# Moving row gathers between the stages of a hybrid decoder layer on one Trainium2 core

## The chip, the cores and the metric

The kernel runs on one core of one Trainium2 chip. The core has a matrix engine (TensorE, PE in the profile, with its weight load PEld), a vector engine (VectorE, DVE), a scalar engine (ScalarE, ACT), GpSimd (POOL) and a queue engine (SyncE, SP). The metric is device microseconds (us) of one execution, as the median of several runs; lower is better.

## The reference

One decoder layer is applied to 512 prompt tokens and to 64 sample tokens (8 sequences of 8). Cut to what matters here:

- `proj = x @ w_in` gives q, k, v, u and two gates. Sliding-window attention runs on q, k, v and a state-space branch on u.
- `mix = sigmoid(ga) * (a @ w_attn_proj) + sigmoid(gb) * (s @ w_ssm_proj)`, then `x = LN1(alpha * x + mix @ w_out)`.
- `peer`: for each token, 8 heads choose 16 of 16,384 experts by product keys (`q = x @ w_q`, two top-16 lists, the top 16 of their sums). With the chosen indices, `h = gelu(x . u_tab[idx])` and `y = sum(g * h * v_tab[idx])`. Then `x = LN2(alpha * x + y)`.
- A last gated addition, `x = x + sigmoid(x @ w_gate) * (p @ w_proj)`.

All tensors are float32.

## The kernel before

**Two groups of tokens.** Group A is the 64 sample tokens (block 0) and the first 128 prompt tokens (block 1). Group B is the other 384 prompt tokens (blocks 2, 3 and 4). Group A goes through attention, state space, output product, norm and expert choice first; group B follows stage by stage.

**Two ways to do the experts.** For group B the expert layer is dense: all 128 "columns" of 128 experts are multiplied on TensorE, first `u` (`up`, L1143), then, weighted by a grid of gates, `v` (L1288). For group A only the chosen rows are read: GpSimd gathers one row of the table for each of the 128 partitions (`gathered`, L1077), and VectorE makes one pass over it, a product with a sum for `u_tab` (L1087) or a multiply-add into `acc` for `v_tab` (L1096). Block 1 has 128 rows of each table, block 0 has 64 of each: 384 row steps, in one fixed order (block 1 u, block 1 v, block 0 u, block 0 v). Four buffers hold gathered rows (`gt`, 4), so a gather waits until the pass four rows earlier is done.

**How row steps are placed.** `rows` is that chain of row steps and `pull(n)` adds n to a running debt and performs a row step for each whole unit of it. Each stage of group B calls `pull` at its own steps. The constants say how much each call asks for: `PG` in the gated linear unit (`glu`, 4 steps), `P0` beside the attention product (`mix0`, 8 steps), `P1` beside the state-space product (`mix1`, 8 steps), `P4` beside the output product (`out`, 8 steps, L655), `P2` beside the norm (`ln1`, 3 steps), `P3` beside the expert query (`peerq`, 4 steps, L426), `PULL1` beside each of the first 50 u columns (`first`). In `dense` 78 columns do u and v together and ask for `PULL3` each (in three thirds), and the last 50 do only v and ask for `PULL4` each.

**What sets the order.** The instructions of an engine are issued in one order fixed at compile time by a planner; the passes over rows are pinned (`pin`) behind what was traced before them on VectorE, other instructions can move forward. The matrix engine works on float32 as a high and a low part (`split`, `parts`): ScalarE copies the high part (L214), VectorE subtracts to get the low part (L217, `wl`, `ul`, `vl`), and three products are summed. The first `W1` = 8 columns of `first` take the raw float32 table instead, with no split. Beside the columns of `first`, two steps per column of `side` run on VectorE: the close of the top-k of block 2 (11 steps), 8 empty steps, 17 steps of its gate grid, and the same for blocks 3 and 4. So the side work is done after about 47 columns.

**The tail.** After the dense stage each block is normed and goes through the gate product (`ple`, L1383), in the order 1, 2, 3, 4, 0. Before the norm of block 0 there are six calls `pull(2)` and then, in `norm(0)`, `pull(1000)`, which performs all row steps that are left; then `acc` of block 0 is folded on TensorE (L1102), added (L1103) and normed.

```
tail = (1, 2, 3, 4, 0)
norm(2)
for i, bi in enumerate(tail):
    pull(PULL5)
    if i + 2 < 5 and tail[i + 2]:
        norm(tail[i + 2])
    next(todo[bi])
    pull(PULL6)
    if i == LASTN:
        norm(0)
...
```

Of the kernel before, what the change touches and what calls it, by code (L numbers as in the profile page):

```python
# [36 lines left out]
E0 = 50  # L37
EB, KB, TB = 2, 2, 2
BQ, ABG, AB0, AB1, AB2 = 2, 0, 1, 1.5, 2
P0, P1, P2, P3, P4, PG = 0.75, 1.5, 3, 2, 1.5, 1  # L40
YFIRST = True
QK0, QK1 = (4, 0, 1), (2, 3)
SIDE = 2
# [3 lines left out]
W0, W1, WHOLEQ, DEEP = 0, 8, 1, 2  # L47
# [6 lines left out]
T0, T1, T2 = 0.5, 1, 1  # L54
LATE = 0
AHEAD = 3
PULL1, PULL3, PULL4, PULL5 = 0.75, 3, 1, 2

# [140 lines left out]
def build(tc, I, O, dbg=None):  # L201
# [17 lines left out]
    with (  # L219
# [889 lines left out]
        def pull(n):  # L1109

            due[0] += n
            while due[0] >= 1:
                due[0] -= 1
                while rows and next(rows[0], rows) is rows:
                    rows.pop(0)
# [11 lines left out]
        def up_parts(e2, du, whole=False, deep=3):  # L1127

            raw = du.tile([128, D], FP, tag="ur", name="ur", bufs=3)
            SY.dma_start(raw, I["u_t"][e2].rearrange("p c e -> p (c e)"))  # L1130
            return (raw,) if whole else split(du, raw, D, "u", deep)

        def up(e2, u, x, hp, tag="gl", bufs=5, lanes="AB"):

            xh, xl, xr = x
            p = ps(384, lanes[e2 % len(lanes)])
            if len(u) == 1:
                terms = ((u[0], xr, True, True),)
            else:
                terms = ((u[0], xh, True, False), (u[0], xl, False, False), (u[1], xh, False, True))  # L1140
            for w, z, f, l in terms:
                for c in range(8):
                    T.matmul(p, w[:, c * 128:c * 128 + 128], z[:, c], start=f and c == 0, stop=l and c == 7)  # L1143
            gl = hp.tile([128, 384], FP, tag=tag, name="gl", bufs=bufs)
            act(gl, p, AF.Gelu)
            return gl
# [59 lines left out]
        def first(du, hp, oh, x, topk):  # L1206

            io16 = oh.tile([128, 128, 2], F16, name="io16")
            V.tensor_copy(io16, iota[:, :, None].to_broadcast([128, 128, 2]))

            def side():
                for b in range(3):
                    while 2 + b not in GW:
                        next(topk, 0)
                        yield

                    for _ in range(LAG[b]):
                        yield
                    yield from grid(b, oh, io16)

            work = side()
            def parts_of(e2):
                return up_parts(e2, du, W0 <= e2 < W1, DEEP)


            u = parts_of(0)
            for e2 in range(E0):
                u, now = parts_of(e2 + 1) if e2 + 1 < E0 else None, u
                if e2 < KEEP:
                    H0[e2] = up(e2, now, x, hp, "keep", KEEP, lanes="A")  # L1230
                else:
                    SY.dma_start(Hd[e2], up(e2, now, x, hp, lanes="A"))
                for _ in range(SIDE):
                    next(work, 0)
                pull(PULL1)
            for _ in work:
                pull(PULL1)

# [309 lines left out]
        with tc.tile_pool(name="hp", bufs=1) as hp:  # L1548
            with tc.tile_pool(name="du", bufs=1, reuse_waits="tile") as du, tc.tile_pool(name="oh", bufs=1) as oh:
                first(du, hp, oh, x, B.topk(tk, (0, 1, 2)))  # L1550
            xrs.close()
            tks.close()
            du2 = ExitStack()
            du = open_(du2, "du2", 1, "right", reuse_waits="tile")

            def last():
                du2.close()
                xB.close()
                return finish(open_(fin, "fin", 1, "right"))

            dense(du, hp, x, last)
# [17 lines left out]
```

## Time and profile before

| | |
|---|---|
| median of 3 runs | 1870.27 us (1869.79 to 1870.85) |
| profiled execution, its own time | 1867.68 us |
| its span, first to last instruction | 1865.9 us |
| mean granted TensorE clock | 0.979 |
| PE busy | 1791.8 us (96%) |
| DVE busy | 1451.8 us (78%) |
| ACT busy | 756.8 us (41%) |
| POOL busy | 575.1 us (31%) |

The profile is of one execution. An engine's busy time is the sum of its instructions' times; what matters for an edit is the engine that ends a wait in the stage where the edit is. A granted clock of 1.0 is TensorE's upper level (2.4 GHz), 0.5 the lower (1.2 GHz); a stretch in between has some time at each.

### The profile page before, as it was taken

The numbers are of one execution on the slowest core, as the hardware profiler recorded it, in microseconds if no ns is written. First come the engines' busy times: TensorE is split into PE (matmuls) and PEld (weight loads), VectorE is DVE, ScalarE is ACT, GpSimd is POOL, SyncE is SP. The second block draws the span as 40 slices with busy tenths as digits, with TensorE's granted clock in tenths as the row PEclk, the third lists the DMA queues.
The fourth block names the chain that finished last, engine by engine and source line by source line (L and its number), as shares of the span: only waits on it lengthen the run. The fifth ranks groups of instructions, "written<-read, shape, count | busy, mean of one in ns | idle before, by whom it ended". The sixth has DMA issues, their size and how long they took to land.

```text
span 1865.9 us, 26455 instructions
## 1 busy us (share of the span) xinstructions
PE 1791.8 (96%) x9506; PEld 1539.1 (82%) x9506; DVE 1451.8 (78%) x2878; ACT 756.8 (41%) x1135; POOL 575.1 (31%) x409
## 2 busy tenths in 40 slices
PE   8799999999989989999999999999999999899997
PEld 6778987767769678889889999999999998688885
DVE  7553343796769999899778888888888887898885
ACT  1213452242243259697743333333333333443331
POOL 0110000032321121112245655555555554542230
PEclk9898999999999989999999999999999999999998
DMA  8824564167883469898999999999999999999952
GB/s 254 302 97 140 157 225 161 58 220 242 307 324 139 148 209 286 276 310 285 304 381 375 387 338 340 348 337 348 337 344 346 334 327 343 402 368 365 337 165 82
DMA packets 212226, 515.43 MB, mean 276 GB/s; under 512 B 33536, under 2 KB 101648, under 8 KB 211568
## 3 DMA queue, kind: packets, MB, share of 16 engines
q1 hardware_dynamic: 145648, 301.68, 46.5%
q0 software_dynamic: 56160, 204.78, 30.2%
q10 hardware_dynamic: 10288, 7.30, 1.3%
q8 instruction: 74, 1.21, 0.3%
q14 instruction: 56, 0.46, 0.1%
HBM read 463.31 MB, written 51.89 MB: 276 GB/s over the span
## 4 chain that ended last, share of the span: by engine, by line
PE 51%; issue 15%; DVE 14%; DMA 11%; POOL 7%; ACT 2%; SPq 0%; ACTq 0%; POOLq 0%; DVEq 0%
PE psA L1288 9%; PE psB L1288 9%; POOL g L1077 7%; PE psA L1143 7%; PE psA L419 6%; PE psB L1143 5%; DMA g<-u_tab,idx 4%; PE psA L426 3%; DMA g<-v_tab,idx 3%; DVE eq L217 3%; PE psB L419 2%; DVE scr L1087 1%; DVE ul L217 1%; PE psA L655 1%; ACT Gs L211 1%
## 5 line engine op out<-in xcount | busy, mean ns | idle before, releaser
L1077 POOL DMA_INDIRECT g<-u_tab,idx x192 | 274.0, 1427 | 792.5 <-DVE scr L1087 485.2
L1077 POOL DMA_INDIRECT g<-v_tab,idx x192 | 282.5, 1471 | 325.9 <-DVE acc L1096 259.8
L1087 DVE SCALAR_TENSOR_TENSOR scr<-g,x 128x1024 bf16<-128x1024 f32 x192 | 233.9, 1218 | 27.0 <-DMA g<-u_tab,idx 25.9
L1096 DVE SCALAR_TENSOR_TENSOR acc<-g,hh,acc 128x1024 f32<-128x1024 f32 x190 | 243.2, 1280 | 10.6 <-DMA g<-v_tab,idx 9.1
L214 ACT ACTIVATE uh<-ur 128x1024 fp32r<-128x1024 f32 x120 | 126.7, 1062 | 163.8 <-PE psA L1143 68.6
L214 ACT ACTIVATE vh<-vr 128x1024 fp32r<-128x1024 f32 x128 | 135.9, 1061 | 96.7 <-PE psB L1288 88.0
L217 DVE TENSOR_TENSOR ul<-ur,uh 128x1024 fp32r<-128x1024 f32 x120 | 146.0, 1217 | 29.7 <-ACT uh L214 29.7
L214 ACT ACTIVATE wh<-wt 128x384 fp32r<-128x384 f32 x128 | 67.1, 524 | 233.5 <-PE psB L1288 200.5
L217 DVE TENSOR_TENSOR vl<-vr,vh 128x1024 fp32r<-128x1024 f32 x128 | 155.9, 1218 | 4.2 <-ACT vh L214 4.2
L1288 PE MATMUL psA<-vh,wh 128*128 128x512 f32 x384 | 150.5, 392 | 8.5 <-ACT wh L214 8.5
L1288 PE MATMUL psA<-vl,wh 128*128 128x512 f32 x384 | 150.7, 393 | 0.0
L1288 PE MATMUL psB<-vl,wh 128*128 128x512 f32 x384 | 150.7, 392 | 0.0
L1288 PE MATMUL psB<-vh,wh 128*128 128x512 f32 x384 | 150.1, 391 | 0.0
L1288 PE MATMUL psB<-vh,wl 128*128 128x512 f32 x384 | 149.9, 390 | 0.0
L1288 PE MATMUL psA<-vh,wl 128*128 128x512 f32 x384 | 149.5, 389 | 0.0
L217 DVE TENSOR_TENSOR wl<-wt,wh 128x384 fp32r<-128x384 f32 x128 | 71.2, 556 | 96.1 <-PE psB L1288 88.4
L1143 PE MATMUL psA<-xh,ul 128*128 128x384 f32 x648 | 132.7, 342 | 4.5 <-DVE ul L217 4.5
L1143 PE MATMUL psA<-xh,uh 128*128 128x384 f32 x648 | 134.3, 346 | 2.5 <-ACT uh L214 2.4
L419 PE MATMUL psB<-xTB,w 128*128 128x384 f32 x400 | 133.7, 486 | 0.0
L1143 PE MATMUL psA<-xl,uh 128*128 128x384 f32 x648 | 128.5, 338 | 0.0
L1143 PEld LDWEIGHTS psA<-xh,uh 128*128 128x128 f32 x648 | 115.9, 192 | 7.8 <-ACT uh L214 3.6
L1143 PEld LDWEIGHTS psA<-xh,ul 128*128 128x128 f32 x648 | 113.8, 190 | 7.4 <-DVE ul L217 5.8
(367 smaller groups left out, 3534.4 us busy)
## 6 DMA issues: line engine op xcount, KB each, us to landing
ur<-u_t SPq DMA_DIRECT2D x128, 512.0 KB
vr<-v_tab SPq DMA_DIRECT2D x128, 512.0 KB
G<-Gg SPq DMA_DIRECT2D x33, 768.0 KB
Gg<-Gs SPq DMA_DIRECT2D x12, 2048.0 KB
w<-w_in SPq DMA_DIRECT2D x42, 512.0 KB
w<-w_q SPq DMA_DIRECT2D x32, 512.0 KB
Hd<-gl SPq DMA_DIRECT2D x48, 192.0 KB
gl<-Hd SPq DMA_DIRECT2D x48, 192.0 KB
```

What stands on the lines that cost most here:

```text
L211: S.activation(out, in_, fn, **k)
L214: S.activation(out, in_, AF.Copy)
L217: return (e or V).tensor_tensor(out, a, b, op=op)
L419: T.matmul(out, w[:, k, :], x[:, k, :], start=(k == 0), stop=(k == kc - 1))
L426: T.matmul(out, a[:, k], b[:, k], start=f and k == 0, stop=l and k == kc - 1)
L655: T.matmul(p[bi][:n], a[:, k + i, c0:c0 + n], b[:, i], start=f and i == 0, stop=e and i == 1)
L1077: G.indirect_dma_start(out=t, out_offset=None, in_=I[tab], in_offset=bass.IndirectOffsetOnAxis(ap=IDX[bi][:, i:i + 1], axis=0))
L1087: pin(V.scalar_tensor_tensor(scr, t, 1.0, X1[bi], op0=mult, op1=mult, accum_out=hh[:, i:i + 1]))
L1096: pin(V.scalar_tensor_tensor(acc, t, hh[:, i:i + 1], acc, op0=mult, op1=add))
L1143: T.matmul(p, w[:, c * 128:c * 128 + 128], z[:, c], start=f and c == 0, stop=l and c == 7)
L1288: T.matmul(y[b][hf], x[:, bs], z[:, hf * 512:hf * 512 + 512], start=f, stop=l)
```

## The change

Five constants change, and in `first` the row steps beside the u columns become conditional.

```diff
-P0, P1, P2, P3, P4, PG = 0.75, 1.5, 3, 2, 1.5, 1
+P0, P1, P2, P3, P4, PG = 1, 1.5, 1, 2, 1, 1
...
-PULL1, PULL3, PULL4, PULL5 = 0.75, 3, 1, 2
+PULL1, PULL3, PULL4, PULL5 = 1, 3, 1, 2
...
                 for _ in range(SIDE):
                     next(work, 0)
-                pull(PULL1)
+
+                pull(PULL1 if e2 >= W1 + 4 else 0)
             for _ in work:
                 pull(PULL1)
```

The attention product asks for 1 row step per step instead of 0.75, the output product for 1 instead of 1.5, the norm for 1 instead of 3. Beside the u columns 0 to 11 no row step is asked for, beside columns 12 to 49 one each instead of 0.75. Nothing else changes: the 384 row steps and their order are the same.

## Rows read from the trace of the kernel before

**Rows 1.** The page's list of engines: busy us, share of the span, instructions.

```profile
PE 1791.8 (96%) x9506; PEld 1539.1 (82%) x9506; DVE 1451.8 (78%) x2878; ACT 756.8 (41%) x1135; POOL 575.1 (31%) x409
```

**Rows 2.** Busy time by stretch: PE, PEld, DVE, ACT, POOL, granted clock, DMA share, GB/s.

```profile
418.00:474.00 56.00, 55.73 (x218) 39.45 (x217) 33.08 (x53) 12.43 (x20) 16.52 (x13) 1.00 0.74 246
493.00:513.00 20.00, 18.01 (x65) 14.40 (x66) 16.47 (x27) 3.40 (x3) 7.31 (x7) 0.83 0.86 275
533.00:545.00 12.00, 4.69 (x21) 3.96 (x21) 4.98 (x8) 3.65 (x4) 3.81 (x4) 0.88 1.01 400
545.00:580.00 35.00, 35.00 (x203) 33.98 (x202) 25.04 (x106) 12.32 (x17) 3.35 (x2) 0.94 0.47 180
666.00:716.00 50.00, 43.36 (x279) 41.57 (x278) 50.00 (x128) 29.24 (x34) 10.63 (x7) 0.86 0.63 210
716.00:930.00 214.00, 205.26 (x1535) 188.28 (x1534) 191.96 (x299) 171.77 (x264) 43.17 (x28) 0.99 0.90 297
```

**Rows 3.** Timeline of PE, output product: start, us, engine, line, operands, [idle before <- releaser].

```profile
494.99 1.22 PE L655 MATMUL psA<-wl,mh 128*128 128x512 f32 x2 [2.94 <-DVE wl L217]
...
501.13 0.67 PE L655 MATMUL psA<-wl,mh 128*128 128x512 f32 x2
```

**Rows 4.** Timeline of DVE, output product: passes over rows, and the low part.

```profile
477.27 1.22 DVE L1087 SCALAR_TENSOR_TENSOR scr<-g,x 128x1024 bf16<-128x1024 f32 x1
...
478.53 1.23 DVE L1087 SCALAR_TENSOR_TENSOR scr<-g,x 128x1024 bf16<-128x1024 f32 x1
...
490.22 1.23 DVE L1087 SCALAR_TENSOR_TENSOR scr<-g,x 128x1024 bf16<-128x1024 f32 x1 [2.16 <-DMA g<-u_tab,idx]
...
493.72 1.22 DVE L217 TENSOR_TENSOR wl<-w,wh 128x1024 fp32r<-128x1024 f32 x1
```

**Rows 5.** Timeline of PE, then DVE, at the start of the expert query.

```profile
543.79 1.65 PE L426 MATMUL psA<-xh,wl 128*128 128x384 f32 x4 [5.68 <-DVE wl L217]
...
541.36 1.23 DVE L1087 SCALAR_TENSOR_TENSOR scr<-g,x 128x1024 bf16<-128x1024 f32 x1 [2.52 <-DMA g<-u_tab,idx]
...
542.51 1.22 DVE L217 TENSOR_TENSOR wl<-w,wh 128x1024 fp32r<-128x1024 f32 x1
```

**Rows 6.** Timeline of ACT there: high parts, and the load that one waited for.

```profile
533.94 1.05 ACT L214 ACTIVATE wh<-w 128x1024 fp32r<-128x1024 f32 x1
...
538.47 1.06 ACT L214 ACTIVATE wh<-w 128x1024 fp32r<-128x1024 f32 x1 [3.48 <-DMA w<-w_q]
```

**Rows 7.** Timeline of PE after the eight raw u columns.

```profile
672.71 2.93 PE L1143 MATMUL psA<-xh,ul 128*128 128x384 f32 x8 [3.26 <-DVE ul L217]
...
693.20 0.59 PE L1174 MATMUL psB<-oa,o 128*128 128x128 f16 x4 [3.38 <-DVE oa L217]
```

**Rows 8.** Waits between 716 and 930: us, times, longest.

```profile
DVE ul L217 <- ACT uh L214: 13.8, 5, 5.3
```

**Rows 9.** Groups on DVE between 1790 and 1830: count, busy, mean ns, idle before.

```profile
L1096 DVE SCALAR_TENSOR_TENSOR acc<-g,hh,acc 128x1024 f32<-128x1024 f32 x12 | 15.4, 1279 | 0.8 <-DMA g<-v_tab,idx 0.7
```

**Rows 10.** Timeline of POOL: a gather beside the norm, and the last gather.

```profile
527.09 0.94 POOL L1077 DMA_INDIRECT g<-u_tab,idx  x1 [16.06 <-DVE scr L1087]
...
1817.29 0.94 POOL L1077 DMA_INDIRECT g<-v_tab,idx  x1 [0.30 <-issue]
```

**Rows 11.** Timeline of DVE: passes after these two gathers, and block 0's norm.

```profile
533.09 1.23 DVE L1087 SCALAR_TENSOR_TENSOR scr<-g,x 128x1024 bf16<-128x1024 f32 x1 [0.43 <-DMA g<-u_tab,idx]
...
1827.01 1.28 DVE L1096 SCALAR_TENSOR_TENSOR acc<-g,hh,acc 128x1024 f32<-128x1024 f32 x1 [0.74 <-DMA g<-v_tab,idx]
...
1838.26 1.28 DVE L1067 SCALAR_TENSOR_TENSOR x<-x,rs,nb 128x1024 f32<-128x1024 f32 x1
```

**Rows 12.** Timeline of PE around the fold of block 0.

```profile
1828.35 3.78 PE L1102 MATMUL psB<-acc,c_fold 128*128 128x512 f32 x4 [1.81 <-DVE acc L1096]
...
1838.98 1.98 PE L1383 MATMUL psA<-w_gatel,th 128*128 128x512 f32 x8
...
1858.03 1.98 PE L1383 MATMUL psB<-w_gateh,tl 128*128 128x512 f32 x8
```

## Prediction

> **What bounds the kernel now.** I read the page first: TensorE (PE) is busy 1791.8 us of the 1865.9 us span [rows 1], so the edit can win only where PE waits or runs at the lower clock, and can lose wherever a new wait reaches PE. Then the busy time by stretch, to find those places. PE is nearly full beside the attention and state-space products, where VectorE has 17 us to spare in 56 (418 to 474). It is not full in three stretches beside which row steps stand today [rows 2]: the output product (493 to 513: PE 18.0 of 20, clock 0.83), the start of the expert query behind the norm (533 to 545: PE 4.7 of 12; then clock 0.94 for 35 us), and the first split u columns (666 to 716: PE 43.4 of 50, clock 0.86, VectorE 50.0 of 50). Last the timelines of these stretches and of the tail, to see which instruction ended each wait.
>
> The reader is to see one pattern. PE's wait ends with a VectorE instruction (`wl`, `ul`, `oa`) that had its input long before and stood behind passes over gathered rows. In the output product PE waits 2.94 us for `wl` and runs slowly until about 501 [rows 3]; in front of that `wl` stands a pass that itself waited for its gather [rows 4]. In the query PE waits 5.68 us for a `wl` that starts at 542.51, though its high part was there at about 535; a pass that waited 2.52 us for its gather stands between [rows 5, 6]. Behind the raw columns PE waits 3.26 us for `ul` and 3.38 us for `oa` [rows 7].
>
> **How many row steps move.** From the constants: before, glu 4, attention 8 x 0.75 = 6, state space 12, output 12, norm 9, query 8, u columns 50 x 0.75 = 37.5, dense 78 x 3 + 50 = 284; together 372.5. The tail's six calls of 2 add 12, which is 384.5 for 384 steps, and the trace shows just 12 passes in the tail [rows 9]: `pull(1000)` finds nothing. After: 4 + 8 + 12 + 8 + 3 + 8 + 38 + 284 = 365, plus 12 is 377. Seven row steps are left for `pull(1000)`, in front of the fold of block 0. So the edit does two things: it clears VectorE's queue at three places, and it puts seven gathers with their passes into the tail.
>
> **Cost, part by part.** A u pass takes VectorE 1.26 us from start to start [rows 4], a v pass 1.28 [rows 9]. Each moves 128 x 1024 floats, 0.52 MB, from GpSimd's queue.
>
> *Attention product, two more steps:* 2.5 us of VectorE, in front of a stretch with 17 us (VectorE's) and more of cover [rows 2]. Zero; without that cover 2.5.
>
> *Output product, four fewer:* until the late `wl` the number done is the same 28 (4 + 8 + 12 + 4 against 4 + 6 + 12 + 6), but two of them now run earlier, in spare time, so the ring of four gathers is no longer drained and the wait of 2.16 us before `wl` goes. PE's 2.94 us and about 2.5 us of slow running (0.17 of the clock over the stretch's first 15 us) go: I take -5, at least -1, at most -5.5.
>
> *Norm, six fewer:* 7.6 us of passes and their waits leave the queue in front of the query's first `wl`. It can then start at 535, when its input is there. PE's 5.68 us and 0.06 of 35 us, 2.1 us, are to be had; next late is the load of the following `w_q`, which ScalarE awaited 3.48 us [rows 6]; six gathers of 0.52 MB fewer, while the DMA engines were full at 400 GB/s [rows 2], bring it earlier. I take -7, between -2 (that load binds) and -7.8.
>
> *Columns 0 to 11, nine fewer:* 11.3 us of VectorE where VectorE is never idle. PE's loss there is 6.6 us idle and 0.14 of 43 us, 6 us: 12.7. The first wait goes with its slow running; the second shrinks only by what VectorE gains over PE, which arrives earlier too. I take -8, between -4 and -12.
>
> *Columns 12 to 49, 9.5 more:* 12 us of VectorE, 5 MB of gathers. From 716 to 930 VectorE has 22 us to spare of 214 and PE 9 [rows 2]; much of VectorE's spare time comes from waiting for ScalarE's high parts [rows 8] and can take passes, but it is not spread evenly. The bounds are 0 and 12; I take +3, a quarter, since the largest waits there are not VectorE's making.
>
> *The tail, seven more:* pulled in one go, they stand in VectorE's pinned order between the last pass at 1827.01 and the fold at 1828.35 [rows 11, 12]. The ring has four buffers: the thirteenth gather can't start before the ninth pass is done, and so on. From a gather's start to its pass, where the pass waited for the data, the trace shows 6.0 us (527.09 to 533.09) and 9.7 us (1817.29 to 1827.01) [rows 10, 11]. Chaining seven steps through four buffers with 6.0 us ends the last pass 12.6 us later than now, with 9.7 us 20.0 us later; at VectorE's own pace, 7 x 1.28, it would be 9.0. I take 14.5, that of 7 us, because little else loads in the tail. PE is in order, and now does half a block of the gate product behind the fold [rows 12]. While it waits it can at most do what needs neither the fold nor the norm of block 0; the chain from fold to the end of that norm is 11.1 us (1828.35 to 1839.5) and block 0's own products 11, so no more than some 4.5 us of the delay can be won back. I take 3: +11.5, between +4.5 and +20.
>
> The Trainium skill speaks for a cheaper tail: DMA: Bandwidth & Descriptors, section "Anatomy of one DMA — SWDGE (gpsimd) path", gives a gather issued by GpSimd 2.0 us and its bytes at 436 GB/s, an estimate of 3.2 us for 0.52 MB. By that the flush would go at VectorE's pace (the first rival below). The trace doesn't agree: 6.0 us is the shortest wait shown here.
>
> **Sum.** -5 - 7 - 8 + 3 + 11.5 = -5.5 us. The profiled execution took 1867.68 us, with 1.8 us around its span; the median of the runs is 2.6 us above it. 1867.7 - 5.5 = 1862.2, and on the median 1864.8: **1865 us**.
>
> **Rivals.**
> 1. *The flush goes at VectorE's pace.* Seven passes at 1.28, less 4.5 won back, is +4.5. For it: only two gathers were in flight at the last wait, and nothing forbids the planner to put other products ahead of the fold. Against it: the 6.0 and 9.7 us. -20 + 3 + 4.5 = -12.5: 1858. Chance 0.14.
> 2. *The tail costs more than the front wins (slower).* The seven gathers land at the tail's 9.7 us and PE's order stays: 20 us of waiting, and 2 more for restarting at the lower clock, as after the waits at 494.99 and 672.71 [rows 3, 7]. -17 + 22 = +5: 1875. It decides as soon as the last pass comes over 17 us later and nothing is won back. Against it: the 9.7 us had an output write beside it. Chance 0.15.
> 3. *The 38 columns become VectorE's.* All 12 us show: -20 + 12 + 11.5 = +3.5, 1874. For it: VectorE is busy 90% there. Against it: its spare 22 us. Chance 0.10.
> 4. *The gain behind the norm isn't there,* since the `w_q` loads end the wait anyway: -2 in place of -7, so -0.5, 1870. Chance 0.11.
>
> My forecast has the rest, 0.50, and by itself lies between 1860 and 1869.
>
> **How the numbers follow.** A measurement of this kernel can tell about 0.2%, 3.7 us, from no change. Four fifths of the forecast's cases and all of the first rival's are faster by more than that: 0.54. The rest of the forecast's (0.10), the fourth rival and the milder ends of rivals 2 and 3 (0.06) lie within it: 0.27. The remaining 0.19 is slower. The range runs from below the first rival, 1856, to just above the second, 1876.
>
> **What would show each step.** In the profile after: no PE wait for `wl` in the output product and at the query's start, and a granted clock near 1 through both; PE arriving at the raw columns about 12 us earlier; the wait for `ul` behind them gone, that for `oa` smaller; dense beginning some 17 us earlier than now; 19 passes instead of 12 in the tail, with a PE wait for `acc` at L1102 of some 10 us in place of 1.81. The prediction is wrong if dense doesn't begin at least 10 us earlier, if the waits only move to another VectorE instruction in the u columns, or if the fold's delay is far from 14 us. The sum is a difference of two larger numbers, 17 and 11.5, so an error of a third in either turns faster into no change.

## The result, and the profile after

The changed kernel takes 1882.41 us (median of 4 runs, 1881.27 to 1884.62), the kernel before 1870.03 beside it: a ratio of 1.0080, 95% interval 1.0063 to 1.0097. The forecast was 1865 us and faster. The profiled execution took 1881.27 us with a span of 1879.5, 13.6 us more than the span before.

The page's list of engines for the kernel after; its line answers to [rows 1]:

```profile
PE 1789.4 (95%) x9506; PEld 1536.5 (82%) x9506; DVE 1453.7 (77%) x2878; ACT 756.7 (40%) x1135; POOL 571.1 (30%) x409
```

The engines do the same work in a longer span, so the 13.6 us are waits of PE. Where they lie is read from busy time by stretch (columns as in [rows 2]), after. PE arrives about 7 us earlier from the output product on, so these stretches are shifted by as much:

```profile
486.00:506.00 20.00, 20.00 (x88) 16.16 (x87) 15.29 (x22) 5.16 (x5) 6.37 (x6) 1.00 0.89 314
528.00:540.00 12.00, 6.07 (x33) 5.75 (x33) 4.66 (x4) 4.08 (x5) 0.00 (x0) 0.94 1.02 401
540.00:575.00 35.00, 35.00 (x198) 33.98 (x198) 20.95 (x103) 11.15 (x16) 0.00 (x0) 0.92 0.25 86
659.00:709.00 50.00, 41.87 (x287) 39.67 (x287) 49.57 (x121) 35.08 (x47) 3.36 (x2) 0.90 0.50 165
709.00:923.00 214.00, 200.18 (x1471) 182.80 (x1469) 194.39 (x298) 163.94 (x249) 54.20 (x36) 0.97 0.91 306
```

The first line is the success: the output product has no gap and the full clock, where it had 18.0 of 20 and 0.83. The `wl` that started at 493.72 [rows 4] now starts at 487.91 (timeline of VectorE), with two passes fewer in front of it. The last pass ahead of it still waits for its gather:

```profile
486.75 1.22 DVE L1087 SCALAR_TENSOR_TENSOR scr<-g,x 128x1024 bf16<-128x1024 f32 x1 [1.58 <-DMA g<-u_tab,idx]
...
487.91 1.22 DVE L217 TENSOR_TENSOR wl<-w,wh 128x1024 fp32r<-128x1024 f32 x1
```

The other stretches are no success: the start of the query still has PE idle for half of 12 us and a clock of 0.92 behind it, the first split u columns are no better than before (41.9 of 50 against 43.4), and in the later columns PE has lost 5 us (200.2 of 214 against 205.3). VectorE is still hardly ever idle in the first split columns (49.6 us of 50), though nine passes in front of them are gone.

The waits themselves, from the timeline of PE after (query, first split columns):

```profile
539.41 1.65 PE L714 MATMUL psB<-w,ev 128*128 128x128 f32 x6 [5.35 <-ACT ev L214]
...
663.37 1.70 PE L1143 MATMUL psA<-xh,uh 128*128 128x384 f32 x8 [3.73 <-ACT uh L214]
...
685.89 0.27 PE L1174 MATMUL psB<-oa,o 128*128 128x128 f16 x1 [2.96 <-DVE oa L217]
```

In [rows 5] and [rows 7] PE waited 5.68 us for `wl` and 3.26 us for `ul`, both VectorE's. Both have gone, and a wait of nearly the same length stands at the same place, now for ScalarE: 5.35 us for `ev`, 3.73 us for `uh`. The timeline of ScalarE after shows what stands in front of these two:

```profile
531.20 1.06 ACT L214 ACTIVATE wh<-w 128x1024 fp32r<-128x1024 f32 x1 [2.67 <-DMA w<-w_q]
535.02 1.06 ACT L214 ACTIVATE wh<-w 128x1024 fp32r<-128x1024 f32 x1 [2.76 <-DMA w<-w_q]
537.93 1.06 ACT L214 ACTIVATE wh<-w 128x1024 fp32r<-128x1024 f32 x1 [1.85 <-DMA w<-w_q]
538.89 0.47 ACT L214 ACTIVATE ev<-psA 128x384 f32<-128x384 f32 x1
...
660.79 1.59 ACT L214 ACTIVATE PFx<-PF 128x1664 uint16<-128x1664 uint16 x1 [5.84 <-DVE PF L1010]
662.28 1.04 ACT L214 ACTIVATE uh<-ur 128x1024 fp32r<-128x1024 f32 x1
```

ScalarE takes its instructions in the order that the planner fixed. `ev`, a copy of 0.47 us, stands behind three high parts that each wait for a load of `w_q`. The first split column's `uh` stands behind `PFx`, a copy for the top-k that waits 5.84 us for VectorE. In the kernel before the same two instructions stand the other way round: the timeline of ScalarE before has that `uh` first and the next `PFx` 7 us behind it.

```profile
663.60 1.06 ACT L214 ACTIVATE uh<-ur 128x1024 fp32r<-128x1024 f32 x1 [0.54 <-DMA ur<-u_t]
...
670.84 1.59 ACT L214 ACTIVATE PFx<-PF 128x1664 uint16<-128x1664 uint16 x1 [5.80 <-DVE PF L1010]
```

In the tail, the timelines of VectorE, GpSimd and PE after answer to [rows 10 to 12]; 19 passes stand there in place of the 12 of [rows 9]:

```profile
1829.25 2.61 DVE L1096 SCALAR_TENSOR_TENSOR acc<-g,hh,acc 128x1024 f32<-128x1024 f32 x2 [0.91 <-DMA g<-v_tab,idx]
1832.90 1.33 DVE L1096 SCALAR_TENSOR_TENSOR acc<-g,hh,acc 128x1024 f32<-128x1024 f32 x1 [1.04 <-DMA g<-v_tab,idx]
1835.62 1.28 DVE L1096 SCALAR_TENSOR_TENSOR acc<-g,hh,acc 128x1024 f32<-128x1024 f32 x1 [1.39 <-DMA g<-v_tab,idx]
...
1839.31 2.60 DVE L1096 SCALAR_TENSOR_TENSOR acc<-g,hh,acc 128x1024 f32<-128x1024 f32 x2 [0.61 <-DMA g<-v_tab,idx]
...
1834.50 0.94 POOL L1077 DMA_INDIRECT g<-v_tab,idx  x1 [0.59 <-DVE acc L1096]
...
1841.97 3.78 PE L1102 MATMUL psB<-acc,c_fold 128*128 128x512 f32 x4 [15.66 <-DVE acc L1096]
```

The fold waits 15.66 us for `acc` in place of 1.81 [rows 12] and comes 13.6 us later. Behind it nothing is won back: from the fold to the end of PE's last product it is 31.6 us after and 31.7 before.

### The profile page after: what moved, and what is told of

Same layout as the page of the kernel before. It is cut to its first block, busy times and chain, and to the rows that moved or that the text cites. A ratio compares the mean times of both kernels' runs of the same rounds, so it can differ in the third digit from the quotient of the medians.

```text
span 1879.5 us, 26465 instructions
## 1 busy us (share of the span) xinstructions
PE 1789.4 (95%) x9506; PEld 1536.5 (82%) x9506; DVE 1453.7 (77%) x2878; ACT 756.7 (40%) x1135; POOL 571.1 (30%) x409
## 4 chain that ended last, share of the span: by engine, by line
PE 49%; issue 3%; ACT 2%; DMA 2%; DVE 2%; POOL 1%; POOLq 0%; DVEq 0%; ACTq 0%
PE psA L1143 13%; PE psA L1289 12%; PE psB L1289 12%; PE psB L1143 8%; ACT Gs L211 1%; POOL g L1077 1%; DMA fr<-w_gate 1%; PE psB L1384 1%; PE psA L1384 1%; PE psB L1175 1%; DMA g<-v_tab,idx 1%; PE psB L1174 1%; ACT ob L211 1%; DMA g<-u_tab,idx 0%; ACT uh L214 0%
## 5 line engine op out<-in xcount | busy, mean ns | idle before, releaser
L1077 POOL DMA_INDIRECT g<-u_tab,idx x192 | 269.2, 1402 | 816.1 <-DVE scr L1087 510.9
L1087 DVE SCALAR_TENSOR_TENSOR scr<-g,x 128x1024 bf16<-128x1024 f32 x192 | 234.5, 1221 | 18.6 <-DMA g<-u_tab,idx 17.4
L214 ACT ACTIVATE wh<-wt 128x384 fp32r<-128x384 f32 x128 | 67.1, 524 | 232.5 <-PE psB L1289 197.5
L1143 PE MATMUL psA<-xl,uh 128*128 128x384 f32 x648 | 133.4, 344 | 0.0
## 6 DMA issues: line engine op xcount, KB each, us to landing
Hd<-gl SPq DMA_DIRECT2D x48, 192.0 KB, 4.2
gl<-Hd SPq DMA_DIRECT2D x48, 192.0 KB, 6.0
```

The lines of the kernel that those rows point to most:

```text
L214: S.activation(out, in_, AF.Copy)
L1077: G.indirect_dma_start(out=t, out_offset=None, in_=I[tab], in_offset=bass.IndirectOffsetOnAxis(ap=IDX[bi][:, i:i + 1], axis=0))
L1087: pin(V.scalar_tensor_tensor(scr, t, 1.0, X1[bi], op0=mult, op1=mult, accum_out=hh[:, i:i + 1]))
```

## The experiments

Most runs move row steps by the same constants; e9, e10 and e13 to e16 also change something else, which their edits show. The table is worked out from the timelines of PE, one profiled execution each: **front** from the first product of the output product to the first raw u product, **u** from there to the first v product, **uv** to the last u product of dense, **v** to the last v product, **fold** to the fold of block 0. All medians are beside a median of before of 1867.0 to 1868.7 us on the same chip (1870.0 for the changed kernel). How far a stage repeats is read from the kernels that leave it as it was: front from 147.9 to 152.5, u from 314.6 to 317.3, uv from 611 to 615 with no link to an edit. So a difference of 3 us or less in u, or of 4 to 5 us or less in front and uv, is not read as an effect.

| kernel | median, ratio [95%] | front | u | uv | v | fold |
|---|---|---|---|---|---|---|
| before | 1870.0 (with after) | 151.4 | 317.2 | 614.4 | 234.1 | 37.5 |
| after | 1882.4, 1.0080 [1.0063, 1.0097] | 144.8 | 326.9 | 611.2 | 235.2 | 50.4 |
| e1_rows_back | 1875.1, 1.0031 [1.0012, 1.0049] | 144.3 | 324.5 | 614.4 | 241.8 | 36.8 |
| e2_tail_alone | 1879.9, 1.0055 [1.0036, 1.0074] | 151.0 | 314.6 | 614.8 | 232.5 | 51.1 |
| e3_front_alone | 1869.4, 1.0003 [0.9990, 1.0015] | 144.5 | 315.8 | 614.1 | 243.1 | 36.8 |
| e4_columns_alone | 1873.4, 1.0027 [1.0009, 1.0044] | 147.9 | 324.0 | 614.1 | 231.2 | 35.5 |
| e5_front_dense | 1861.0, 0.9967 [0.9953, 0.9980] | 144.7 | 316.8 | 614.6 | 233.2 | 36.8 |
| e6_columns_0_11 | 1869.5, 1.0005 [0.9991, 1.0019] | 151.6 | 321.2 | 611.4 | 233.9 | 36.9 |
| e7_columns_12_49 | 1889.7, 1.0124 [1.0103, 1.0144] | 152.1 | 336.2 | 611.1 | 233.5 | 37.0 |
| e8_after_dense | 1870.9, 1.0012 [1.0001, 1.0024] | 144.8 | 323.7 | 613.4 | 233.5 | 36.8 |
| e9_pfx_gpsimd | 1886.8, 1.0108 [1.0085, 1.0131] | 144.2 | 338.2 | 615.0 | 234.4 | 36.8 |
| e10_tail_buffers | 1877.0, 1.0043 [1.0026, 1.0060] | 151.1 | 317.0 | 614.0 | 232.0 | 46.1 |
| e11_tail_half | 1870.7, 1.0015 [1.0001, 1.0029] | 149.7 | 315.1 | 614.2 | 230.8 | 43.0 |
| e12_fewer_in_columns | 1864.8, 0.9977 [0.9968, 0.9987] | 144.5 | 318.0 | 610.9 | 239.5 | 36.8 |
| e13_half_passes | 1870.2, 1.0014 [1.0004, 1.0024] | 152.5 | 321.3 | 610.9 | 233.6 | 37.0 |
| e14_half_gathers | 1864.9, 0.9987 [0.9975, 0.9998] | 150.2 | 318.6 | 610.9 | 235.5 | 36.8 |
| e15_side_later | 1869.9, 1.0004 [0.9990, 1.0018] | 148.3 | 318.5 | 612.1 | 234.5 | 36.8 |
| e16_side_later_best | 1860.7, 0.9959 [0.9944, 0.9974] | 143.1 | 314.6 | 615.0 | 234.0 | 37.1 |
| e17_norm_alone | 1868.0, 0.9998 [0.9980, 1.0017] | 149.5 | 315.8 | 614.5 | 234.4 | 37.1 |
| e18_out_alone | 1862.9, 0.9977 [0.9958, 0.9996] | 144.9 | 317.3 | 613.9 | 234.6 | 36.8 |

**The tail, undone and alone.** On the changed kernel (e1), then on the kernel before (e2):

```diff
-PULL1, PULL3, PULL4, PULL5 = 1, 3, 1, 2
+PULL1, PULL3, PULL4, PULL5 = 1, 3, 1.15, 2
...
-PULL1, PULL3, PULL4, PULL5 = 0.75, 3, 1, 2
+PULL1, PULL3, PULL4, PULL5 = 0.75, 3, 0.86, 2
```

> The changed kernel with PULL4 raised from 1 to 1.15, so that the seven left-over row steps stand beside the last 50 v columns and the tail has its 12 passes again. Theory of the tail (all the loss is the flush of seven rows in front of the fold): the wait for acc at L1102 goes from 15.7 us back to about 2, the fold comes about 13.6 us earlier and the time is 1882.4 - 13.6 = 1869, no change against before. Rival (VectorE has no room in the v columns either): seven passes at 1.28 us push the dense end back by up to 9 us, and the time is 1875 to 1878.

> The kernel before with PULL4 lowered from 1 to 0.86, so that seven row steps are left for the flush in front of the fold, and nothing else. Theory of the tail: the fold waits about 15 us for acc, and the time is 1870 + 13.6 = 1884, as slow as the changed kernel or slower. Rival (the loss comes from the stages in front, and the flush only shows it): a few us, 1871 to 1876.

The tail alone, on an untouched front, makes the kernel slower by 0.55%. Its fold stage grows by 13.6 us, as in the changed kernel (12.9); by the median the loss is 11 us, less than the 14 expected. Putting the seven rows back beside the last 50 v columns takes that away, but the v stage grows by 7.7 us: the rival's price, about 1.1 us a row. Busy time by stretch of the kernel before shows what is full there:

```profile
1560.00:1660.00 100.00, 91.53 (x390) 74.13 (x389) 87.02 (x113) 42.62 (x55) 44.27 (x25) 0.97 1.01 399
```

The DMA engines are at 1.01 and 399 GB/s. Among the waits from 1560 to 1790, ScalarE's for the v table's load was 7.9 us before; with seven more rows (e1) it is:

```profile
ACT vh L214 <- DMA vr<-v_tab: 29.0, 13, 5.1
```

**The front alone, the u columns alone.** Both on the kernel before: e3 takes the three constants of the changed kernel and leaves `PULL1` at 0.75, with eight rows put beside the v columns; e4 takes the edit of the u columns alone (`PULL1` 1 and the condition).

```diff
-P0, P1, P2, P3, P4, PG = 0.75, 1.5, 3, 2, 1.5, 1
+P0, P1, P2, P3, P4, PG = 1, 1.5, 1, 2, 1, 1
-PULL1, PULL3, PULL4, PULL5 = 0.75, 3, 1, 2
+PULL1, PULL3, PULL4, PULL5 = 0.75, 3, 1.16, 2
...
-PULL1, PULL3, PULL4, PULL5 = 0.75, 3, 1, 2
+PULL1, PULL3, PULL4, PULL5 = 1, 3, 1, 2
-                pull(PULL1)
+                pull(PULL1 if e2 >= W1 + 4 else 0)
```

> The kernel before with P0, P2 and P4 of the changed one, PULL1 as before in all 50 columns, and the eight missing row steps put beside the last 50 v columns (PULL4 1.16). Theory that the changed columns give the lead back: the 6.5 us won in the output product last to the end, 1863.5. Rival (the split u columns wait for VectorE whatever comes before, so that an earlier arrival is only waited away): 1868 to 1870.

> The kernel before with the edit of the u columns alone: no row step beside columns 0 to 11, one beside each of the other 38, so that the tail has 11 passes and no flush. Theory that the changed columns give the lead back (the profile after goes from 6.9 us ahead at the raw columns to 2.8 us behind at dense): 9.7 us slower than before at the start of dense, 1879. Rival (the lead is lost in waits that are there without the edit): within 3 us of before, 1867 to 1873. The prediction's own terms, -8 for columns 0 to 11 and +3 for the others, give 1865.

By the median e3 looks like its rival, no gain. Its stages say otherwise: 6.9 us are won in front and kept through u and uv, and 8.9 us are lost in the v columns, where the eight rows went. e4's u stage is 6.8 us longer: the changed columns lose time by themselves, though less than the 9.7 expected.

**The same rows in the first part of dense.** e5 is e3 with the rows moved again; e8 is the changed kernel with its seven rows there.

```diff
-PULL1, PULL3, PULL4, PULL5 = 0.75, 3, 1.16, 2
+PULL1, PULL3, PULL4, PULL5 = 0.75, 3.1, 1, 2
...
-PULL1, PULL3, PULL4, PULL5 = 1, 3, 1, 2
+PULL1, PULL3, PULL4, PULL5 = 1, 3.1, 1, 2
```

> Like the run of the front alone, but the eight missing row steps stand beside the 78 columns of dense that do u and v (PULL3 3.1, PULL4 1). Theory (the front's 6.3 us reach the end unless rows are put where the DMA engines are full, as in the first v columns): the lead of 6.6 us stands at the last u column and at the fold, 1862. Rival (dense has no room either): the eight passes cost 8 x 1.28 us or more there, 1868 to 1872.

> The changed kernel with PULL3 raised from 3 to 3.1, so that the seven left-over row steps stand in the first part of dense and nothing is left for the flush. If the flush is worth 11 to 14 us and dense has room: 1882 - 13 = 1869 to 1871. If dense has no room: 1876 to 1880.

No cost of eight more rows is to be seen there (614.6 against 614.4), and e5 beats both kernels. e8 is the changed kernel without its flush: 11.5 us faster than it by the medians, and 9.9 us slower than e5, from which it differs in the u columns alone (6.9 us by their u stages).

**The two parts of the u columns apart,** on the kernel before, the balance in the first part of dense:

```diff
-PULL1, PULL3, PULL4, PULL5 = 0.75, 3, 1, 2
+PULL1, PULL3, PULL4, PULL5 = 0.75, 3.12, 1, 2
-                pull(PULL1)
+                pull(PULL1 if e2 >= W1 + 4 else 0)
...
-PULL1, PULL3, PULL4, PULL5 = 0.75, 3, 1, 2
+PULL1, PULL3, PULL4, PULL5 = 1, 2.88, 1, 2
-                pull(PULL1)
+                pull(PULL1 if e2 >= W1 + 4 else 0.75)
```

> The kernel before with no row step beside u columns 0 to 11 and 0.75 beside the other 38 as before; the nine row steps stand in the first part of dense (PULL3 3.12). The prediction's term: 8 us earlier at dense, 1861. Theory that nothing is won there (the wait for VectorE turns into one for ScalarE's high part, behind the top-k): dense starts within 3 us of before and the time is 1867 to 1872. Rival that these columns carry the loss: dense starts 4 us or more later.

> The kernel before with one row step beside each of u columns 12 to 49 in place of 0.75, columns 0 to 11 as before; ten row steps fewer in the first part of dense (PULL3 2.88). The prediction's term: dense starts 3 us later. Theory that these columns are full: dense starts 8 to 12 us later and the time is 1878 to 1882 (some of it won back if dense gains from ten rows fewer). Rival: no effect, 1869.

Clearing the first twelve columns makes u 4.0 us longer, not 8 shorter. None of that stands at the first split column. Its first product comes 45.2 us behind the first raw product in e6 and 41.1 before, but in the kernel before the wait for `ul` still follows [rows 7]. With it the column ends at 50.5 us before, and at 51.2 in e6; PE's wait for the first `oa` ends at 68.1 before and at 67.7 in e6. VectorE has come no further either: in the first 67 us it makes 8 passes before and 2 in e6, yet it is idle for no more than 2.1 us and starts that `oa` only 0.4 us earlier. Other work, moved forward by the planner, stands where the passes stood. The 4 us come later. The first two lines are PE's waits for `oa` in e6 (first raw product at 631.91), at the gate grids of blocks 2 and 3; the last is the one at block 3 in the kernel before (625.14):

```profile
699.64 0.26 PE L1174 MATMUL psB<-oa,o 128*128 128x128 f16 x1 [2.96 <-DVE oa L217]
...
789.92 0.41 PE L1174 MATMUL psB<-oa,o 128*128 128x128 f16 x4 [3.59 <-DVE oa L217]
...
781.55 0.23 PE L1174 MATMUL psB<-oa,o 128*128 128x128 f16 x1 [1.19 <-DVE oa L217]
```

At block 3 e6 is 1.6 us behind (158.0 us from the first raw product against 156.4), and the rest is lost in the columns after it. Why is not shown.

Ten more rows beside columns 12 to 49 cost 19 us on top of the nine in front of them, and 2.5 us (e8 against e6) to 5.7 (after against e6) where those nine are gone. The 19 us are more than the 8 to 12 of the theory, and e7's profiled execution is its shortest (1882.25 us, median 1889.69). The waits of PE in e7 from 716 to 930:

```profile
PE psA L1143 <- ACT uh L214: 15.7, 8, 6.2
PE psB L1174 <- ACT Gs L211: 4.9, 9, 0.7
```

and the busy time of that stretch in e7:

```profile
716.00:930.00 214.00, 188.80 (x1399) 171.65 (x1398) 192.70 (x305) 157.36 (x235) 50.18 (x33) 0.98 0.87 295
```

PE has lost 16 us of busy time there, VectorE is no busier than in [rows 2], and PE waits for ScalarE (for `uh` 2.4 us in the kernel before). The longest of these waits, on the timelines of ScalarE and SyncE in e7:

```profile
741.54 1.06 ACT L214 ACTIVATE uh<-ur 128x1024 fp32r<-128x1024 f32 x1 [4.42 <-DMA ur<-u_t]
...
725.35 8.79 SPq L1232 DMA_DIRECT2D Hd<-gl  x2
734.23 0.98 SPq L1130 DMA_DIRECT2D ur<-u_t  x2
```

`uh` waited for its table load, and that was issued at 734.23, behind writes of finished columns on which SyncE's queue had stood since 725.35. So a late column delays its own write and, behind it, the load of a later column.

**VectorE or the gathers' traffic?** On e7: the 38 passes of columns 12 to 49 over half of each row (e13), then their gathers halved too (e14). Both kernels leave out half of these 38 products.

```diff
+                F["half"] = e2 >= W1 + 4
                 pull(PULL1 if e2 >= W1 + 4 else 0.75)
+            F["half"] = False
...
+                w = 512 if F.get("half") else D
-                pin(V.scalar_tensor_tensor(scr, t, 1.0, X1[bi], op0=mult, op1=mult, accum_out=hh[:, i:i + 1]))
+                pin(V.scalar_tensor_tensor(scr[:, :w], t[:, :w], 1.0, X1[bi][:, :w], op0=mult, op1=mult, accum_out=hh[:, i:i + 1]))
...
-                G.indirect_dma_start(out=t, out_offset=None, in_=I[tab],
+                h = F.get("half")
+                G.indirect_dma_start(out=t[:, :512] if h else t, out_offset=None,
+                                     in_=I[tab].rearrange("n (a b) -> (n a) b", a=2) if h else I[tab],
```

> The kernel with one row step beside each of u columns 12 to 49 and 0.75 beside the first twelve, whose 38 passes in columns 12 to 49 now take only half of each row (512 of 1024 elements; the other half of these products is left out), with the gathers whole. If VectorE's time is the cause of the 19 us: 38 x 0.6 = 23 us less of it, the raw columns to the first dense product go from 336 back to about 316 us, and the time from 1889 to 1869. If the gathers' traffic is the cause: 332 us or more, 1885.

> As the run with half passes, and the gathers of these 38 rows bring only 512 elements each (half rows; the other half of the products is left out as before). If the gathers' traffic delays the table loads: another 5 us or more off the stretch from the raw columns to dense. If VectorE's time is all: the same as with half passes, within 3 us.

Half the passes' time brings 14.9 of the 19 us back, half the gathers' bytes another 2.7, within what u repeats to. PE's wait for `uh` from 716 to 930 falls from 15.7 to (e13, whose line numbers are one higher):

```profile
PE psA L1144 <- ACT uh L214: 1.1, 2, 0.6
```

So most of the 19 us is VectorE's time, which by the waits shown reaches PE through ScalarE's and SyncE's queues. Not all: e13's 38 half passes of 0.69 us take less of VectorE than the 28 whole ones of 1.22 us in these columns before, 26 us against 34, and u is still 4.1 us longer. What that rest is was not tested further. Fewer passes than before win nothing, as e12 shows (e5 with 0.5 in place of 0.75 row steps beside columns 12 to 49, and `PULL3` 3.22):

> The version with the changed front alone and eight more rows in dense, and now 0.5 in place of 0.75 row steps beside u columns 12 to 49 (9 fewer), which go into dense too (PULL3 3.22). If VectorE sets the pace of these columns in proportion (ten more rows cost 20 us): 10 us or more faster than 1861, 1850. If its spare time there hides 0.75 a column, and only more than that costs: 1861. If dense is full by now: 1863 to 1868.

u is 318.0 us against 316.8. That its v stage is 6 us longer isn't explained.

**Why clearing columns 0 to 11 wins nothing.** e9 is e8 with the copy `PFx` of group B on GpSimd, so that it can't stand in front of `uh`. e15 is e6, and e16 is e5, with the side work begun more slowly:

```diff
-                        copy(PFx, PF[:, hs_, :, None].to_broadcast(sh))
+                        (G.tensor_copy if bi > 1 else copy)(PFx, PF[:, hs_, :, None].to_broadcast(sh))
...
-LAG = (8, 2, 2)
+LAG = (0, 2, 2)
-                for _ in range(SIDE):
+                for _ in range(SIDE if e2 >= W1 else 1):
```

> Like the changed kernel with its seven rows in dense, but the copies PFx of group B's top-k (12 of 1.59 us) are made by GpSimd and no longer by ScalarE. Theory (in the changed kernel TensorE waits at the first split column for ScalarE's high part, which stands behind a PFx that waits for the top-k on VectorE): the wait of 3.3 to 3.7 us for uh there goes, dense starts some 4 us earlier, 1867. Rival (without it the wait is VectorE's again, for ul or oa): nothing is won, 1870 to 1873.

> The kernel with no row steps beside columns 0 to 11 (nine more in dense), and one side step in place of two beside columns 0 to 7; eight empty side steps of block 2 are left out, so that the side work ends in the same column. Theory (clearing the first columns only lets the top-k stand ahead of the first split column's high part in ScalarE's order): the wait of 3.7 us for uh goes and the stretch from the raw columns to dense takes 312 to 316 us in place of 321, 1860 to 1864. Rival (the top-k's work on VectorE has to be done anyway and only comes later): 318 to 322 us, 1867 to 1872.

> The best version so far (the front alone, eight more row steps in dense, 1861) with the same later side steps, row steps beside columns 0 to 11 kept. If VectorE's queue in front of the first split column sets the loss there (3.3 us for ul, 3.4 for oa): 4 to 6 us faster, 1856. Rival: the work only moves, 1861.

In e9 the wait for `uh` at the first split column is gone, and PE stands at the next product of that column (timeline of PE):

```profile
669.71 1.65 PE L1143 MATMUL psA<-xh,ul 128*128 128x384 f32 x4 [6.89 <-DVE ul L217]
```

That is the rival's outcome, a longer wait for VectorE. The 14 us that e9 loses in u go further than either theory. GpSimd's copies take 1.6 to 3.3 us each and share its queue with the gathers; that this is the cause is not shown. In e15 PE still waits 3.29 us for `uh` behind the same `PFx`, so the theory that later side steps would put `uh` first falls. e16 equals e5.

**The flush.** e10 is e2 with seven buffers of their own for the last seven rows; e11 is the kernel before with three rows left (`PULL4` 0.95).

```diff
-                t = gt.tile([128, D], FP, tag="g", name="g")
+                t = F.get("gt2", gt).tile([128, D], FP, tag="g", name="g")
...
+                        F["gt2"] = open_(fin, "gt2", 7, "right")
                         pull(1000)
```

> The kernel with the tail alone changed (seven rows left for the flush), with seven gather buffers of their own for these seven rows. If the ring of four buffers sets the flush, as the prediction had it: the gathers start at once, the passes follow at VectorE's 1.28 us, and the wait for acc goes from 15.9 us to some 8, 1872 to 1874. If the landing of the gathers sets it, whatever the buffers: 1879 to 1880, no change.

> The kernel before with PULL4 0.95: three row steps are left for the flush in place of seven. If each row costs the same (11.4 us at the fold for seven): 4.9 us at the fold, 1873. By the ring of four with 6 us from a gather to its pass: the first three gathers follow the passes nine to eleven one round trip later, 6 us or more at the fold, 1875. At VectorE's pace: 3.8 us, 1872.

With its own buffers the flush has no wait for data left; this line on VectorE in e10 holds two passes of the tail's twelve and the seven:

```profile
1824.97 11.84 DVE L1096 SCALAR_TENSOR_TENSOR acc<-g,hh,acc 128x1024 f32<-128x1024 f32 x9
```

The fold stage is 46.1 us: 8.6 us over before, where seven passes at VectorE's 1.28 are 9.0. With the ring of four it was 13.6 over. So the ring costs 5 us of the flush and the passes the rest. Three rows cost 5.5 us, which fits both a price per row (5.8) and one round trip; e11 doesn't tell these apart. Its median is only 0.15% over before; of the difference its v stage, with three rows fewer, shows 3.3 us (230.8 against 234.1).

**The front's two parts,** on the kernel before, the balance in dense (`PULL3` 3.08 and 3.03):

```diff
-P0, P1, P2, P3, P4, PG = 0.75, 1.5, 3, 2, 1.5, 1
+P0, P1, P2, P3, P4, PG = 0.75, 1.5, 1, 2, 1.5, 1
...
-P0, P1, P2, P3, P4, PG = 0.75, 1.5, 3, 2, 1.5, 1
+P0, P1, P2, P3, P4, PG = 1, 1.5, 3, 2, 1, 1
```

> The kernel before with P2 lowered from 3 to 1 alone, the six row steps moved into the first part of dense (PULL3 3.08). The prediction's term: the query's products end 7 us earlier, and the time is 1861. Theory (ScalarE's high parts of w_q, which wait for their loads, end the wait instead): from the end of the output product to the raw u columns it takes as long as before, 111 us, and the time is 1868, no change. Between them: 2 us won.

> The kernel before with P0 1 and P4 1 alone (two more row steps beside the attention product, four fewer beside the output product), P2 as before, two row steps more in dense (PULL3 3.03). Theory: the output product ends 6.5 us earlier and keeps it to the end, 1861 to 1862, as the version with the whole front. Rival (the pass beside the norm takes the lead back): 1865 to 1868.

e18 has the whole gain of the front (144.9) and keeps it. In e17 PE's wait for `wl` at the query is replaced as in the changed kernel (timeline of PE):

```profile
545.38 1.52 PE L714 MATMUL psB<-w,ev 128*128 128x128 f32 x6 [4.70 <-ACT ev L214]
```

From the end of the output product to the raw columns it takes 109.4 us in e17, 111.7 before, 111.2 in the changed kernel and 111.3 in e18. In all runs together it takes 110.7 to 112.4 where the norm isn't changed and 109.4 to 111.2 where it is, so the norm wins some 1 us, at most 3, and e17's median shows no gain.

## Why the prediction was wrong

Its terms against the profile after, whose stages give -6.5 in front, +9.8 in u, -2.1 in dense, +12.9 at the fold, and -0.5 around them: +13.6. The step that failed most is the price of the u columns, then that of the norm.

- **Attention and output product (0 and -5):** right. The wait for `wl` and the slow running went; the output product itself, from its first product to its last, takes 33.6 us in place of 39.7, -6.1, half a microsecond past the bound that was given. The bound was small because the lost clock of 0.17, a mean over 20 us [rows 2], was counted over 15; over 20 it is 3.4 us, and 2.94 + 3.4 = 6.3 holds the measured value. The wait for a gather in front of the late `wl` did not go, it is 1.58 us, but no longer reaches PE. VectorE's spare time beside the attention product is 23 us (56 - 33.1), not 17: the prediction took the column of PEld, which changes nothing in the zero. This edit alone gives the front's gain (e18).
- **Norm (-7):** failed. The step "it can then start at 535" counted the wait for VectorE as the price. The prediction had seen that ScalarE awaited `w_q` for 3.48 us [rows 6], and put -2 as the end where that binds; it does. It is -0.5 in the changed kernel, -2.3 in e17. Rival 4 was right on this term. That six gathers fewer would bring the load earlier didn't help: between 528 and 540 the DMA engines are still full (1.02, 401 GB/s).
- **Columns 0 to 11 (-8):** failed, and in sign. "The first wait goes with its slow running" looked at VectorE's queue alone. With the passes gone, ScalarE has `PFx` in front of `uh`, and that waits for VectorE's top-k: a wait of 3.73 us for `uh` replaces the 3.26 us for `ul`. The time that the passes left on VectorE went to other work, so that the wait for `oa` ends only 0.4 us earlier (e6), and nothing is won up to there. The +4.0 us come behind that, from the grid of block 3 on, and their cause stays open. The prediction named "the waits only move to another VectorE instruction" as what would make it wrong; they moved to an instruction of ScalarE that waits for VectorE. Why the order of `PFx` and `uh` turned stays open too: slower side steps (e15) didn't turn it back.
- **Columns 12 to 49 (+3, bounds 0 and 12):** the changed kernel's u stage shows 2.5 to 5.7 us, inside the bounds, but only because the nine rows in front are gone. Alone it is 19 us (e7), past the upper bound of 12, which was the passes' own VectorE time. The step that fails is that bound: a late VectorE holds back a column, its write, and through SyncE's queue the next load and its `uh`, so a pass can cost more than its length. How ten passes, 12.6 us, become 19 in full is not settled. Rival 3's mechanism (these columns become VectorE's) is the right one in the main (e13 brings 14.9 of the 19 us back).
- **Tail (+11.5):** right in mechanism, the size 1.4 short. The delay of the fold, 12.9 to 13.6, is inside the 12.6 to 20 of the round trips and near the 14.5 taken; the 3 us to be won back by PE were not, since PE's order around the fold stayed. The Trainium skill (DMA: Bandwidth & Descriptors, section "Anatomy of one DMA — SWDGE (gpsimd) path") would have a gather landed after an estimated 3.2 us and so spoke for VectorE's pace. The trace doesn't agree: from the last gather's issue to a pass that waited for it, it is 5.9 us with three rows left (e11, 1818.31 to 1824.23, a wait of 1.29), and over the whole trace after, the median from a gather's issue to its landing is 7.3 us for `u_tab` and 7.5 for `v_tab`. VectorE's pace came only with more buffers (e10).

The error is 19.1 us (-5.5 forecast, +13.6 measured): 14.8 of it are the u columns (-5 forecast, +9.8 measured), 6.5 the norm, 1.4 the tail, less 1.1 that the output product gave more and 2.6 outside the terms (dense and the stages around). The u columns gave back all that the front won, and the tail's 13 us remained. Rival 2 names that outcome (the tail costs more than the front wins), not its reason: its tail of 22 us didn't come, and the front's 17 didn't either.

## What to carry to other kernels

A wait that ends with one engine's instruction is a price only up to the next thing that is late there: look at what the other operand, the next load and the next engine's in-order queue would show if it were gone, before its whole length is counted. Work that is moved has a price at each place it can go, and they differ: here a row step costs nothing that can be seen beside the first 78 dense columns, 1.1 us beside the v columns where the DMA engines are full, 1.9 us in a flush before the last dependent product, and beside u columns where VectorE is nearly full 1.9 us (e7), but only 0.3 to 0.6 where the columns in front were cleared. Seven steps left over by the constants were worth nearly all of this loss (e8 is 11.5 us faster without them), and the version that has the changed front alone and puts the rows in dense (e5) is 0.33% faster than before.

## What was unexpected of the hardware

The copy of 128 x 1664 uint16 that takes ScalarE 1.59 us took GpSimd from 1.57 to 3.33 us, median 2.43. Ten more passes of 1.26 us made a stretch of 50 columns 19 us longer while VectorE's busy time in it, 716 to 930, was 192.7 us against 192.0 [rows 2], and halving the passes there brought 14.9 us back (e13): in this stretch an engine that is 90% busy set the pace without showing it in its busy time.
